# Weight sums of a Strassen-like decoder trunk, built in DRAM by accumulating transfers

## The chip, the cores and the metric

The kernel runs on one core of a Trainium2 chip. The metric is the device time of one execution, in microseconds (us). The engines are TensorE (PE, matmuls), VectorE (DVE), ScalarE (ACT), GpSimd (POOL) and SyncE (SP). Each runs its own instructions in order and waits on semaphores for the others. SP and POOL issue nearly all DMA transfers, SP the loads and POOL the stores, each in its own queue; 16 DMA engines carry them out.

## The reference

Sequence 1024, width D = 1024, float32. One normalised input h is projected by one weight matrix `w_in`; two gated linear attentions run on parts of it, each is projected by its own 1024 x 1024 matrix, the two are merged by sigmoid gates, and one output projection follows.

```python
h = rms_norm(x, norm_w[l]) * (1.0 + scale[:, None, :]) + shift[:, None, :]
proj = h @ w_in[l]
hq, hf, hi, hz, gq, gk, gv, gz, ga, mg = jnp.split(proj, IN_OFFSETS, axis=-1)
y_h = hgrn2_branch(hq, hf, hi, hz, lb_all[l], hgrn_norm_w[l])
y_g = gla_branch(gq, gk, gv, gz, ga, gla_alpha_w[l], gla_alpha_b[l], gla_norm_w[l])
u_h = y_h @ w_branch[l, 0]
u_g = y_g @ w_branch[l, 1]
mg = jax.nn.sigmoid(mg.reshape(B, T, N_BRANCH, D_MODEL))
merged = mg[:, :, 0] * u_h + mg[:, :, 1] * u_g
x = x + gate[:, None, :] * (merged @ w_out[l])
```

The weights concerned here are `hi` and `gv` (the values of the two attentions), `mg` (two gates) and `w_branch` (two branches), each 1024 x 1024.

## The kernel before

Large matmuls are done in float32r after each operand has been split in a high and a low part (an ACT copy and a DVE subtraction), as three products hi*hi, hi*lo, lo*hi. The square products of 1024 x 1024 use a scheme of Strassen's kind: the matrix is cut in quadrants, and seven products of half size (`PRODUCTS = (1, 2, 5, 3, 6, 7, 4)`) take the place of eight. Four of the seven (`SUMS`: 5, 6, 3, 7) need sums of weight quadrants:

- 7 is the quadrant (0,0) plus (0,1); 5 is (0,1) plus (1,1); 6 is 7 plus (1,1); 3 is 6 plus (1,0). In the second value stage 3 is formed with the opposite sign.

The order of the work: the norm and the modulation with the first projections (`front`), then a list of jobs that `stream.go` runs: the first value stage (`vjobs[0]`, for gv), the gate features of the first attention, the second value stage (`vjobs[1]`, for hi), and the features of the second attention. The attention itself runs as generators beside the jobs (`weave`): each `yield n` lets n units of matmuls pass. A second track of such generators, `stream.back`, does work ahead of its use, one after another: `alpha_side`, `v_sums`, `prepare`, `gate_side`. At the end come four closing stages (`last_stages`: two gates, two branches) and the output stage.

The weight sums are made by DVE. `v_sums` loads the four quadrants of hi in two halves (kk), makes four results of 128 x 1024 each and stores them in DRAM (`vs_d`). `prepare` does so for the four closing stages: 16 blocks, each loaded in two DMAs of 512 KB (`load_blocks`), four additions of 128 x 512 to half a block's sums each (`weight_sums`: lines L1174, L1176, L1178, L1180; the profile counts 16 of each), and four stores to `w_sums`. Later `load_duo` and `Vjob.load` read the sums back as if they were weights.

The engines' order: PE, ACT and DVE follow the program as written in the first part (`manual_schedule`), and behind it a scheduler of the framework orders each engine's instructions, DMAs included, by what they depend on; `held` keeps marked instructions in the order of the program. A DMA of POOL takes one of eight semaphores in turn, and so waits on POOL for the one eight places ahead in POOL's queue to have landed, as well as for those that it depends on.

Other names that the steps below use: `h` are stores of the modulated input (L257), `qk` stores of the first attention's queries and keys (L365), `fx` stores of combined input quadrants (L1719), `v` stores of value products (L1769) that the attentions load back (L975), `yg` stores of the first attention's result (L889).

Of the kernel before, what the change touches and what calls it, by code (L numbers as in the profile page):

```python
# [16 lines left out]
P = 128  # L17
# [72 lines left out]
def hybrid_trunk_kernel(  # L90
# [1065 lines left out]

    w_sums = [[[dp.tile([P, T], F32, name=f"ws{b}{j}{i}") for i in range(4)] for j in range(2)] for b in range(4)]

    summed_up = set()
    paused = [False]  # L1160

    def load_blocks(b, i):
        src = sources[b][i]
        x = [S.get([4, 2, P]) for _ in range(2)]
        for kh in range(2):
            nc.sync.dma_start(x[kh].rearrange("p k a f -> p k (a f)"),
                              src[kh * 512:(kh + 1) * 512, :].rearrange("(k p) f -> p k f", p=P))
        return x

    def weight_sums(b, i, x1, x2):  # L1170
        s1, s2 = S.get([2, 4, P]), S.get([2, 4, P])
        parts = {5: s1[:, 0], 6: s1[:, 1], 3: s2[:, 0], 7: s2[:, 1]}
        add = nc.vector.tensor_add
        held(add(parts[7], x1[:, :, 0], x1[:, :, 1]))  # L1174
        yield 1
        held(add(parts[5], x1[:, :, 1], x2[:, :, 1]))  # L1176
        yield 1
        held(add(parts[6], parts[7], x2[:, :, 1]))  # L1178
        yield 1
        held(add(parts[3], parts[6], x2[:, :, 0]))  # L1180
        for p, q in SUMS.items():
            nc.gpsimd.dma_start(w_sums[b][i // 2][q][:, i % 2 * 512:i % 2 * 512 + 512],  # L1182
                                parts[p].rearrange("p k f -> p (k f)"))
        S.free(x1, x2)
        S.free(s1, s2, sent=True)
        summed_up.add((b, i))

    def prepare():
        todo = [(b, i) for b in range(4) for i in range(4)]
        blocks_of = {}  # L1190
        for n in range(len(todo) + 1):
            while n < len(todo) and (len(S.free_list) < 11 or paused[0]):
                yield 1
            if n < len(todo):
                blocks_of[n] = load_blocks(*todo[n])
            if n:
                yield from weight_sums(*todo[n - 1], *blocks_of.pop(n - 1))
            yield 7

# [56 lines left out]
    def load_duo(b, p, j):  # L1256

        t = raw_w[b, p, j] = S.get([2, 512])
        if p in SUMS:
            assert {(b, 2 * j), (b, 2 * j + 1)} <= summed_up  # L1260
            nc.sync.dma_start(t.rearrange("p a f -> p (a f)"), w_sums[b][j][SUMS[p]])
        else:
# [432 lines left out]
    v_d = [dp.tile([T, D], F32, name=f"v{s}") for s in range(2)]  # L1695
    vs_d = {p: [dp.tile([P, T], F32, name=f"vs{p}{kk}") for kk in range(2)] for p in SUMS}
    summed_v = set()
# [23 lines left out]
    def v_sums():  # L1721

        add = nc.vector.tensor_add
        for kk in range(2):
            while len(S.free_list) < 9:
                yield 1
            y = {}
            for at_ in ((0, 1), (1, 1), (0, 0), (1, 0)):
                y[at_] = S.get([2, 512])
                nc.sync.dma_start(y[at_], w_block(1, *at_, kk))  # L1730
            yield 9
            e = S.get([2, 512])
            held(add(e, y[0, 1], y[1, 1]))
            yield 2
            held(add(y[0, 0], y[0, 0], y[0, 1]))
            yield 2
            held(add(y[0, 1], y[0, 0], y[1, 1]))
            yield 2
            held(nc.vector.scalar_tensor_tensor(y[1, 0], y[0, 1], -1.0, y[1, 0], ALU.mult, ALU.subtract))
            for p, t in ((5, e), (7, y[0, 0]), (6, y[0, 1]), (3, y[1, 0])):  # L1740
                nc.gpsimd.dma_start(vs_d[p][kk], t.rearrange("p a f -> p (a f)"))
            S.free(y[1, 1])
            S.free(e, y[0, 0], y[0, 1], y[1, 0], sent=True)
            summed_v.add(kk)
            yield 2

# [48 lines left out]
    class Vjob:  # L1795
# [13 lines left out]
        def load(self):  # L1809
# [6 lines left out]
            if p in SUMS:  # L1816
                assert kk in summed_v
                nc.sync.dma_start(self.w_raw.rearrange("p a f -> p (a f)"), vs_d[p][kk])
            else:
                nc.sync.dma_start(self.w_raw, w_block(s, *W_AT[p], kk))  # L1820
# [95 lines left out]
    def front():  # L1916
# [57 lines left out]
```

## Time and profile before

| | |
|---|---|
| median of 3 runs | 1201.08 us (1200.2 to 1201.88) |
| the profiled execution | 1201.55 us, its span 1199.8 us |
| granted TensorE clock | 0.998 of full |
| instructions profiled | 20303 |
| DMA over the span | 221.24 MB, 184 GB/s in the mean |

How to read the lines shown further on: a group has line, engine, operation, out<-in, the shapes and the count, then busy us and the mean ns of one, then the engine's idle time just before it and who ended it. A timeline row has start, duration, engine, line and operation, and in brackets the idle time before it and what ended that. `SPq` is SP's queue of DMA issues. A DMA row has the count, the KB of each and the median us from issue to landing. A wait row names who waited, for whom, and the us in total, the times and the longest.

### The profile page before, as it was taken

The page shows a single profiled execution, that of the slowest core. Times are in us where ns is not written, and L with a number is a line of the kernel's source. Part 1 is how long each engine was busy: PE and PEld are TensorE (multiplying, and loading weights), DVE is VectorE, ACT ScalarE, POOL GpSimd, SP SyncE. Part 2 cuts the span into 40 slices and gives each one's busy share as a digit, 9 for nine tenths or more (in the row PEclk, how much of TensorE's full clock was granted, in tenths as well). Part 3 has the DMA queues.
Part 4 walks back from the last instruction along what each step waited for, and adds up shares of the span by engine and source line. Part 5 has one row for each costly group of instructions (what it writes and reads, how often), then busy time and mean ns, then how long its engine had stood idle before and what let it go on. Part 6 is the DMA issues. An engine that isn't in the chain of part 4 may idle for free.

```text
span 1199.8 us, 20303 instructions
## 1 busy us (share of the span) xinstructions
PE 1170.1 (98%) x8137; PEld 951.0 (79%) x8137; DVE 846.3 (71%) x1270; ACT 584.9 (49%) x860; POOL 124.3 (10%) x257
## 2 busy tenths in 40 slices
PE   7999999999999999999999999999999999999997
PEld 6776777888878688888888878778888888878886
DVE  4745667657664955887897798695553866988994
ACT  5674462673455445334433435456643644444554
POOL 4111111000110211111111010001120000000000
PEclk9999999999999999999999999999999999999999
DMA  9745445155474855665565454255688846335523
GB/s 324 262 173 201 150 161 176 52 178 175 167 273 141 296 195 161 209 210 160 173 197 178 130 203 124 78 169 179 225 312 284 285 152 210 125 108 173 171 99 134
DMA packets 150641, 221.24 MB, mean 184 GB/s; under 512 B 8971, under 2 KB 107329, under 8 KB 150546
## 3 DMA queue, kind: packets, MB, share of 16 engines
q1 hardware_dynamic: 132114, 158.37, 42.4%
q0 software_dynamic: 18384, 61.56, 13.3%
q8 instruction: 64, 1.05, 0.4%
q14 instruction: 31, 0.25, 0.1%
q10 hardware_dynamic: 48, 0.01, 0.0%
HBM read 154.37 MB, written 65.54 MB: 183 GB/s over the span
## 4 chain that ended last, share of the span: by engine, by line
PE 65%; issue 20%; DVE 6%; ACT 4%; DMA 3%; POOL 2%; SPq 0%; POOLq 0%; DVEq 0%; ACTq 0%
PE pd L594 16%; PE pd L1330 11%; PE pd L1879 9%; PE sc_ps L1330 6%; PE pm L1330 6%; PE pd L1507 3%; PE pd L386 2%; PE sc_ps L1507 2%; PE pm L1507 1%; PE pm L798 1%; POOL ws L1182 1%; DVE b L212 1%; PE pm L817 1%; DMA b<-in_ada_w_dram 1%; PE sc_ps L386 1%
## 5 line engine op out<-in xcount | busy, mean ns | idle before, releaser
L594 PE MATMUL pd<-b,b 128*128 128x512 f32 x1632 | 393.8, 396 | 0.2 <-ACT b L1762 0.2
L594 PEld LDWEIGHTS pd<-b,b 128*128 128x128 f32 x1632 | 303.0, 189 | 65.8 <-issue 0.7
L1330 PE MATMUL pd<-b,b 128*128 128x512 f32 x720 | 173.2, 392 | 0.6 <-DVE b L1422 0.4
L1879 PE MATMUL pd<-b,b 128*128 128x512 f32 x672 | 162.7, 396 | 7.1 <-DVE b L1790 3.4
L1330 PEld LDWEIGHTS pd<-b,b 128*128 128x128 f32 x720 | 133.9, 188 | 31.2 <-DVE b L1422 0.9
L1879 PEld LDWEIGHTS pd<-b,b 128*128 128x128 f32 x672 | 123.4, 188 | 40.7 <-ACT b L1762 4.0
L212 DVE TENSOR_TENSOR b<-b,b 128x1024 fp32r<-128x1024 f32 x78 | 94.2, 1222 | 48.4 <-ACT b L211 48.1
L1273 DVE TENSOR_TENSOR b<-b,b 128x1024 fp32r<-128x1024 f32 x56 | 68.2, 1221 | 69.2 <-ACT b L1272 53.0
L1272 ACT CAST b<-b 128x1024 fp32r<-128x1024 f32 x56 | 58.4, 1050 | 65.0 <-PE pm L1330 18.1
L211 ACT CAST b<-b 128x1024 fp32r<-128x1024 f32 x78 | 79.8, 1047 | 6.4 <-PE pd L1879 3.0
L1330 PE MATMUL sc_ps<-b,b 128*128 128x512 f32 x324 | 78.7, 391 | 0.4 <-ACT b L1302 0.4
L1330 PE MATMUL pm<-b,b 128*128 128x512 f32 x300 | 72.1, 389 | 0.0
L1330 PEld LDWEIGHTS sc_ps<-b,b 128*128 128x128 f32 x324 | 60.4, 188 | 13.9 <-ACT b L1302 1.1
L1249 ACT CAST b<-b 128x1024 fp32r<-128x1024 f32 x48 | 49.7, 1050 | 43.9 <-PE pd L1330 15.9
L1250 DVE TENSOR_TENSOR b<-b,b 128x1024 fp32r<-128x1024 f32 x48 | 57.7, 1219 | 18.4 <-ACT b L1249 12.2
L1330 PEld LDWEIGHTS pm<-b,b 128*128 128x128 f32 x300 | 56.3, 188 | 11.7
L203 DVE TENSOR_TENSOR b<-b,b 128x1024 fp32r<-128x1024 f32 (+1 forms) x36 | 35.1, 983 | 29.5 <-ACT b L202 29.4
L386 PE MATMUL pd<-b,b 128*128 128x512 f32 x192 | 52.3, 405 | 2.8 <-DVE b L362 1.9
L1182 POOL DMA_DIRECT2D ws<-b x64 | 34.9, 546 | 193.6 <-DVE b L1174 107.4
L703 ACT COPY xb<-b 128x512 f32<-128x512 f32 x48 | 29.7, 621 | 50.8 <-PE sc_ps L683 23.8
L817 PE MATMUL pm<-scT,b 128*128 128x128 f32 x256 | 46.9, 275 | 0.0
L386 PEld LDWEIGHTS pd<-b,b 128*128 128x128 f32 x192 | 34.4, 188 | 15.4 <-DVE b L362 2.9
(317 smaller groups left out, 1699.6 us busy)
## 6 DMA issues: line engine op xcount, KB each, us to landing
b<-in_w_in_dram SPq DMA_DIRECT2D x72, 512.0 KB, 4.3
ws<-b POOLq DMA_DIRECT2D x64, 256.0 KB, 3.9
b<-ws SPq DMA_DIRECT2D x32, 512.0 KB, 4.4
b<-in_x_dram SPq DMA_DIRECT2D x16, 512.0 KB, 4.4
b<-in_ada_w_dram SPq DMA_DIRECT2D x32, 256.0 KB, 6.5
v<-b POOLq DMA_DIRECT2D x32, 256.0 KB, 3.7
b<-v SPq DMA_DIRECT2D x16, 512.0 KB, 5.2
b<-fx SPq DMA_DIRECT2D x16, 512.0 KB, 4.5
```

What stands on the lines that cost most here:

```text
L211: held(nc.scalar.copy(hi, src))
L212: nc.vector.tensor_sub(lo, src, hi.bitcast(F32))
L386: nc.tensor.matmul(accs[f], wg(a, d, f), b[d][:, half * 512:half * 512 + 512], start=(d == 0 and n == 0), stop=(d == KT - 1 and n == 2))
L594: nc.tensor.matmul(ps[0:w, th * 512:(th + 1) * 512], a[:, k, 0:w], b[:, th * 512:(th + 1) * 512], start=(k == 0 and n == 0), stop=(k == KT ...
L817: nc.tensor.matmul(o, vch(ch)[:, vh * P:(vh + 1) * P], scT[:, ch, :], start=True, stop=(ch == 0))
L1249: nc.scalar.copy(hi, src)
L1250: nc.vector.tensor_sub(lo, src, hi.bitcast(F32))
L1272: nc.scalar.copy(hi, t)
L1273: nc.vector.tensor_sub(lo, t, hi.bitcast(F32))
L1330: nc.tensor.matmul(o, a[:, sl], c, start=(p in (1, 5) and kt == 0 and n == 0), stop=(kt == 3 and n == 2), skip_group_check=True)
L1507: nc.tensor.matmul(o, a, b, start=(p in (1, 5) and kt == 0 and n == 0), stop=(kt == 3 and n == 2), skip_group_check=True)
L1879: nc.tensor.matmul(st.bank[i], x_, w_, start=(p in (1, 5) and kk == 0 and a == 0 and n == 0), stop=(kk == 1 and a == 1 and n == 2), skip_g ...
```

## The change

The DVE additions of `v_sums` and `weight_sums` go, and with them their loads and stores through SBUF. In their place POOL issues DMAs from DRAM to DRAM: a copy of the first quadrant into the sum's tile, then a DMA with `accum_op=ALU.add` that adds the second to it there; 6 and 3 begin as copies of the finished 7 and 6. `w_sums` becomes one tile of 128 x 4 x 512 for each stage and product. `v_sums` no longer makes 3 with the opposite sign, so the job that uses it splits it with a factor of -1 (`minus_split`). `v_sums` now stands ahead of `alpha_side`, whose delay goes from 72 to 32.

```diff
+    def minus_split(src):
+        hi, lo = (S.get(list(src.shape[1:]), F32R) for _ in range(2))
+        held(nc.scalar.activation(hi, src, AF.Copy, scale=-1.0))
+        nc.vector.scalar_tensor_tensor(lo, src, -1.0, hi.bitcast(F32), ALU.mult, ALU.subtract)
+        return hi, lo
...
-    w_sums = [[[dp.tile([P, T], F32, name=f"ws{b}{j}{i}") for i in range(4)] for j in range(2)] for b in range(4)]
+    w_sums = [{p: dp.tile([P, 4, 512], F32, name=f"ws{b}{p}") for p in SUMS} for b in range(4)]
...
-    def load_blocks(b, i):
...
-    def weight_sums(b, i, x1, x2):
...
+    CHAIN = ((7, (0, 0)), (7, (0, 1)), (5, (0, 1)), (5, (1, 1)), (6, 7), (6, (1, 1)), (3, 6), (3, (1, 0)))
 
     def prepare():
...
+        for b in range(4):
+            def block(kh, a, b=b):
+                src = sources[b]
+                return [src[i][kh * 512:kh * 512 + 512, a * P:a * P + P] for i in range(4)]
+            done = set()
+            for p, src in CHAIN:
+                while paused[0]:
+                    yield 1
+                first = p not in done
+                done.add(p)
+                if isinstance(src, int):
+                    nc.gpsimd.dma_start(w_sums[b][p], w_sums[b][src])
+                else:
+                    for i, x in enumerate(block(*src)):
+                        x = x.rearrange("(k p) f -> p k f", p=P)
+                        y = w_sums[b][p][:, i].rearrange("p (k f) -> p k f", f=P)
+                        if first:
+                            nc.gpsimd.dma_start(y, x)
+                        else:
+                            nc.gpsimd.dma_start(y, x, accum_op=ALU.add)
+                        yield 1
+                yield 4
+            summed_up.add(b)
...
     def v_sums():
...
+        for p, src in CHAIN:
+            first = p not in done
+            done.add(p)
+            for kk in range(2):
+                if isinstance(src, int):
+                    x = vs_d[src][kk]
+                else:
+                    x = w_block(1, *src, kk)
+                y = vs_d[p][kk]
+                if first:
+                    nc.gpsimd.dma_start(y, x)
+                else:
+                    nc.gpsimd.dma_start(y, x, accum_op=ALU.add)
+                yield 2
...
-                self.w = pinned_split(self.w_raw)
+                self.w = minus_split(self.w_raw) if p == 3 else pinned_split(self.w_raw)
...
-        stream.back.append([alpha_side((2, 3)), 72, 1, 0])
         stream.back.append([v_sums(), 2, 1, 0])
+        stream.back.append([alpha_side((2, 3)), 32, 1, 0])
```

What it does to the order of the instructions, at three places. First POOL's queue around the first stores of h. Before, they follow the setup of the masks:

```order
L564 COPY mask16_750<-mask16_750 32x16 x3
L257 DMA h00_112<-b45_225 128x1024
L257 DMA h01_113<-b50_299 128x1024
L257 DMA h02_114<-b55_399 128x1024
L489 MEMSET b69_659 128x512
L491 DMA b69_659<-in_gla_alpha_w_dram 16x512 x4
L567 MEMSET scT_136 128x1024
L257 DMA h03_115<-b62_501 128x1024
```

Now (line L263 is the old L257; L1727 and L1729 are copies and accumulations of `v_sums`, where `vs70` is product 7, half 0; L1187 is a first copy of `prepare`):

```order
L1727 DMA vs60_813<-vs70_817 16x8192
L1729 DMA vs51_812<-in_w_in_dram 256x1x512
L1727 DMA vs61_814<-vs71_818 16x8192
L1729 DMA vs60_813<-in_w_in_dram 256x1x512
L263 DMA h00_112<-b45_225 128x1024
L1729 DMA vs61_814<-in_w_in_dram 256x1x512
L1727 DMA vs30_815<-vs60_813 16x8192
L1187 DMA ws07_774<-in_w_in_dram 128x4x128
L1727 DMA vs31_816<-vs61_814 16x8192
L1729 DMA vs30_815<-in_w_in_dram 256x1x512
L263 DMA h01_113<-b50_299 128x1024
L1729 DMA vs31_816<-in_w_in_dram 256x1x512
```

The value stage's transfers, and from there on those of the closing stages, have moved ahead of and between the stores of the first part. Second, POOL's queue at the stores of the first value stage's sixth product, which the first attention loads. Before:

```order
L1719 DMA fx40_769<-b123_1317 128x1024
L1769 DMA v0_825<-b135_1405 128x512
L1769 DMA v0_825<-b136_1422 128x512
L1769 DMA v0_825<-b135_1405 128x512
L1719 DMA fx41_770<-b124_1318 128x1024
L1769 DMA v0_825<-b136_1422 128x512
```

Now (L1757 is the old L1769, L1713 the old L1719; `ws37` is stage 3, product 7; L1189 accumulates, L1181 copies a sum):

```order
L1757 DMA v0_809<-b135_1403 128x512
L1757 DMA v0_809<-b136_1421 128x512
L1189 DMA ws37_786<-in_w_branch_dram 128x4x128
L1757 DMA v0_809<-b135_1403 128x512
L1187 DMA ws35_783<-in_w_branch_dram 128x4x128
L1713 DMA fx41_770<-b124_1312 128x1024
L1757 DMA v0_809<-b136_1421 128x512
L1187 DMA ws35_783<-in_w_branch_dram 128x4x128 x3
L1189 DMA ws35_783<-in_w_branch_dram 128x4x128 x3
L1757 DMA v0_809<-b125_1321 128x512
L1189 DMA ws35_783<-in_w_branch_dram 128x4x128
L1181 DMA ws36_784<-ws37_786 16x16384
```

At this place the sums of three closing stages are already ahead, and those of the last one stand between the stores; 103 of the 120 transfers are ahead of the fourth store shown, and all 120 ahead of the first yg store. Third, DVE where the first block's additions of a closing stage stood, in the first attention's fourth head. Before:

```order
L1174 TENSOR_TENSOR b_3685<-b_3560 128x512
L1176 TENSOR_TENSOR b_3684<-b_3560,b_3561 128x512
L1178 TENSOR_TENSOR b_3684<-b_3685,b_3561 128x512
L711 TENSOR_TENSOR b_3357<-b_3357,tot_759 128x8x64
L712 TENSOR_TENSOR b_3355<-b_3355,tot_759 128x8x64
L756 COPY_PREDICATED blk<-mask_750,sc_ps 128x8x16
L1180 TENSOR_TENSOR b_3685<-b_3684,b_3561 128x512
```

Now (lines 6 higher):

```order
L212 TENSOR_TENSOR b_3649<-b_3437,b_3648 128x1024
L717 TENSOR_TENSOR b_3339<-b_3339,tot_759 128x16x32
L717 TENSOR_TENSOR b_3339<-b_3339,tot_759 128x8x64
L718 TENSOR_TENSOR b_3337<-b_3337,tot_759 128x8x64
L762 COPY_PREDICATED blk<-mask_750,sc_ps 128x8x16
```

The attention's own operations stand there alone.

More of the change, by code (lines that the diff above doesn't have):

```diff
@@ L1188, in prepare @@
-    def prepare():
[L1189 to L1198, printed above, removed]
+    CHAIN = ((7, (0, 0)), (7, (0, 1)), (5, (0, 1)), (5, (1, 1)), (6, 7), (6, (1, 1)), (3, 6), (3, (1, 0)))
@@ L1695, in hybrid_trunk_kernel @@
     v_d = [dp.tile([T, D], F32, name=f"v{s}") for s in range(2)]
-    vs_d = {p: [dp.tile([P, T], F32, name=f"vs{p}{kk}") for kk in range(2)] for p in SUMS}
+    vs_d = {p: [dp.tile([P, 2, 512], F32, name=f"vs{p}{kk}") for kk in range(2)] for p in SUMS}
     summed_v = set()
@@ L1721, in v_sums @@
     def v_sums():
-        add = nc.vector.tensor_add
-        for kk in range(2):
[L1725 to L1743, printed above, removed]
+        done = set()
+        for p, src in CHAIN:
[12 more added lines that the diff above has]
+                yield 2
+        for kk in range(2):
             summed_v.add(kk)
-            yield 2
+        yield 2
     class Vstage:
```

28 lines of the change are left out of this document (3 added, 25 removed).

## Prediction

> **What bounds the kernel now.** I read the page's busy shares first, then busy time by stretch and PE's waits where the removed additions stand, and last the DMA queues and the timelines of POOL and SP, because the change swaps DVE work for DMA work on POOL's queue.
>
> ```profile
> span 1199.8 us, 20303 instructions
> PE 1170.1 (98%) x8137; PEld 951.0 (79%) x8137; DVE 846.3 (71%) x1270; ACT 584.9 (49%) x860; POOL 124.3 (10%) x257
> ```
>
> PE is busy for 98% of the span, DVE for 71%. The profiled execution took 1201.55 us with this span in it; the median of the runs shown is 1201.08. The sum below is made against 1201.55. Now the stretches (busy us of each engine, granted clock, DMA share, GB/s):
>
> ```profile
> core 0: us, PE busy (x) PEld busy (x) DVE busy (x) ACT busy (x) POOL busy (x), PEclk, DMA share, GB/s
> 0.00:10.00 10.00, 6.01 (x27) 5.64 (x28) 3.92 (x11) 5.64 (x10) 9.35 (x36) 1.00 0.83 235
> 10.00:50.00 40.00, 36.83 (x192) 27.37 (x192) 23.82 (x49) 20.42 (x39) 5.64 (x23) 1.00 1.05 355
> 50.00:100.00 50.00, 49.80 (x252) 36.65 (x251) 23.16 (x48) 35.36 (x57) 11.21 (x18) 1.00 0.51 177
> 100.00:200.00 100.00, 93.56 (x512) 72.12 (x511) 69.87 (x81) 46.61 (x60) 16.07 (x30) 1.00 0.48 167
> 420.00:700.00 280.00, 279.78 (x2604) 233.98 (x2603) 213.24 (x382) 114.09 (x182) 44.09 (x81) 1.00 0.58 183
> ```
>
> Two things are to be seen. From 10 to 50 us the 16 DMA engines are full (share 1.05), so bytes added there push back loads that PE waits for in order. And from 420 to 700 us, where the sums of the closing stages are made, PE is busy for 279.78 of 280 us. PE's waits (us in total, times, longest), the only one of 420 to 700 us, and then the two largest of 700 to 840 us:
>
> ```profile
> PE pd L594 <- ACT b L1762: 0.2, 1, 0.2
> ```
>
> ```profile
> PE sc_ps L652 <- DVE xb L648: 1.9, 1, 1.9
> PE sc_ps L683 <- DVE blk L666: 1.3, 1, 1.3
> ```
>
> **The change part by part.** *Removed: 72 DVE operations.* Two kinds of the four in the closing stages' sums, and two of the four in the value stage's:
>
> ```profile
> L1178 DVE TENSOR_TENSOR b<-b,b 128x512 f32<-128x512 f32 x16 | 11.1, 692 | 0.0
> ...
> L1174 DVE TENSOR_TENSOR b<-b 128x512 f32<-128x512 f32 x16 | 11.0, 687 | 0.0
> L1733 DVE TENSOR_TENSOR b<-b,b 128x1024 f32<-128x1024 f32 x2 | 2.4, 1220 | 0.0
> ...
> L1735 DVE TENSOR_TENSOR b<-b,b 128x1024 f32<-128x1024 f32 x2 | 2.4, 1218 | 0.0
> ```
>
> That is 64 x 0.69 + 8 x 1.22 = 54 us of DVE work. PE waits 0.2 us in the stretch that holds most of it: matmuls hide it already. The two DVE waits just behind, 1.9 + 1.3 = 3.2 us, may go, since DVE gets there with less in hand. The bounds are 0 and 5 us of gain; I take 4. SP loses 40 block loads and POOL 72 stores of sums that go with the additions; those of the closing stages lie in the same covered stretch, and all of them count nothing. The split with a factor of -1 (third product, value stage) is one ACT and one DVE operation of the same shapes in place of two plain ones, twice: nothing, under DVE's idle 29%. The alphas' side work waits 32 units behind value sums that yield 34, so it starts at 66 units instead of 72: nothing.
>
> *Added: 120 transfers from DRAM to DRAM in POOL's queue.* A closing stage has 8 copies and 16 accumulations of 0.262 MB and 2 copies of 1.049 MB, 8.39 MB in all, and there are four; the value stage has 8 copies and 8 accumulations of 0.524 MB, again 8.39 MB. Written: 5 x 8.39 = 41.9 MB, of which 5 x 4.19 = 21.0 MB accumulate. Prices:
>
> ```profile
> q1 hardware_dynamic: 132114, 158.37, 42.4%
> ...
> b<-in_ada_w_dram SPq DMA_DIRECT2D x32, 256.0 KB, 6.5
> ...
> b<-in_w_in_dram SPq DMA_DIRECT2D x24, 256.0 KB, 3.7
> ```
>
> The first row gives the engines' rate: 158.37 MB in 0.424 x 1199.8 = 509 us, 311 GB/s. So 0.262 MB is 0.84 us of all 16 engines, and the 41.9 MB are 135 us if every transfer were a plain copy. No row shows an accumulation. Below it is bounded by a plain copy, 0.84 us; above by the landing of a 256 KB load amid full engines, 6.5 us, as if nothing ran beside it (undisturbed such loads land in 3.7). An accumulation must also read what it adds to, so it is nearest to two plain passes: I take 1.69 us for 0.262 MB, which adds 21.0 MB / 311 GB/s = 67 us and makes 202 us of engine work. The Trainium skill ("Collectives: The Full Stack", section "The bandwidth ceiling: the fold count and why AG ≠ RS ≠ AR") says that the adder itself costs nothing and its second source read does, with a measured ratio of 1.93 to a copy. By that ratio the 67 would be 63 and the time 1302; no run here shows it yet.
>
> *Where they stand.* The change's rows of POOL show it: the transfers need nothing from the compute engines, so they stand from the program's first microseconds on, between the stores of h, qk, fx and v, and all are ahead of the first yg store. Each step of a sum waits on POOL for the step before it to land, and every store behind it in the queue waits too. Where POOL and SP stand now:
>
> ```profile
> 28.17 0.59 POOL L257 DMA_DIRECT2D h<-b  x1 [13.23 <-ACT b L252]
> ...
> 172.50 0.54 POOL L1769 DMA_DIRECT2D v<-b  x1
> ...
> 199.63 0.54 POOL L1769 DMA_DIRECT2D v<-b  x1 [1.78 <-ACT b L1762]
> 259.31 1.08 POOL L889 DMA_DIRECT2D yg<-b  x2 [59.14 <-DVE b L999]
> ```
>
> ```profile
> 185.97 0.96 SPq L975 DMA_DIRECT2D b<-v  x2
> ```
>
> SP's load of v at 185.97, the last row, needs the store of 172.50, 13 us earlier, and SP's queue is in order: behind this load stand the weights of the next matmuls. SP already waits for stores of v, before such weights (us in total, times, longest):
>
> ```profile
> SPq L576 <- DMA v<-b: 20.9, 3, 7.7
> ```
>
> *The sum at two points.* By the shares above, the engines have done 8.3 + 42.0 + 25.5 + 0.48 x 72.5 = 111 us of work by 172.50, and 124 by 199.63. At the v store of 172.50, 103 transfers stand ahead; the 17 behind it (12 accumulations, 3 small and 2 large copies) are 29 us, so 173 are ahead. With the engines always full that store comes at 111 + 173 = 284, 111 late, less 13 of slack: 98 us on SP. At the last v store only 4 accumulations, 7 us, are behind: 124 + 195 = 319, 119 late; its data are not loaded soon, but the halves of buffers that these stores free are. The delay lies between 98 and 119; I take 108. The start is part of this, not extra: the value stage's 16 transfers, 12.6 MB with the second read, are 40 us of engine work, nearly all of it ahead of the second h store, in the full stretch. Nothing recovers it later, since PE is busy throughout. The sum: 1201.55 + 108 - 4 = 1306. POOL's own issue time (count, busy us, mean ns of one) is covered by these waits:
>
> ```profile
> L1182 POOL DMA_DIRECT2D ws<-b x64 | 34.9, 546 | 193.6 <-DVE b L1174 107.4 <-DVE b L1180 26.2 <-DVE b L1178 18.3
> ...
> L357 POOL DMA_DIRECT2D wga<-in_w_in_dram x1 | 1.0, 958 | 0.0
> ```
>
> The second has as many small rows as any of the new ones; 120 x 0.55 to 0.96 us is 66 to 115 us, under the 319.
>
> **The rivals.** *Accumulating is as cheap as copying.* Then 135 us of work: the v store at 111 + 116 = 227, 54 late, less 13 is 41 on SP; the last one 56 late; the middle, 48, gives 1246. Against it: an accumulation reads twice. If only the start paid (40 us) and everything later found slack, the time would be 1238; the 13 us ahead of the v load speak against that.
>
> *Accumulating is much dearer than two passes.* Each further pass over the 21.0 MB adds 67 us: 1373 with one, 1440 with two. At the upper end, 6.5 us for each 0.262 MB, the accumulations take 64 x 6.5 + 8 x 13 = 520 us instead of 134, and the time is 1306 + 386 = 1692. For it: rows of 512 bytes, and chains in which one transfer waits for the landing of another. Against it: two or more chains are in flight at once, and even 30 steps in series (6 in each of five sums) at 6.5 us are 195 us, less than 319.
>
> *The transfers are hidden, and the kernel is faster.* The gain then stands alone: 1201.55 - 4 = 1198. It decides at the v load: the engines' idle time until then is 172.5 - 111 + 13 = 75 us, so the 103 transfers would have to cost under 75 us, while plain copies alone make 116, or 101 at the 355 GB/s of the full stretch. The shares of 0.51 and 0.48 from 50 us on speak for it, the lack of room by a third against it. The Trainium skill ("DMA: Bandwidth & Descriptors", section "Issuing engines are not separate DMA queues") speaks against it as well: transfers issued by any engine end up on the same 16 and interleave.
>
> **How the numbers follow.** Full engines and about two passes (1275 to 1400): 0.58. Cheap accumulation or only the start (1230 to 1275): 0.17. Dear accumulation (over 1400): 0.20. Hidden: 0.05, most of it faster. I predict the likeliest, 1306. The range 1243 to 1440 reaches from just under the cheap case to two more passes; about 0.05 hidden, 0.04 below and 0.11 above are left out. Faster or slower counts from 0.2%, what a measurement of this kernel can tell from no change: faster 0.04, same 0.01, slower 0.95.
>
> **What would show it.** DMA share near 1 from 5 to some 300 us; the SP load of v near 285; the last v store near 310 to 320; new PE waits in the first 65 us that lead back to loads of ada_w, and one or two of tens of microseconds from 100 to 300 us that lead to a POOL store; DVE busy down by some 54 us with nothing gained for it between the first yg stores and the end. The prediction is wrong if DMA is idle while POOL waits (landing time bounds the chains, not bytes), or if PE runs on while the v stores are late.

## The result, and the profile after

The changed kernel takes 1315.05 us (median of 4 runs, 1314.08 to 1317.65) against 1201.48 for the kernel before on the same chip: ratio 1.0946, 95% interval 1.0933 to 1.096. The prediction was 1306 with a range of 1243 to 1440. The profiled execution has a span of 1312.9 us, 113.1 more than the 1199.8 of before.

The page of the changed kernel: span and busy times, DMA share in 40 slices, and the two big DMA queues (q1 is SP's, q0 POOL's; packets, MB, share of 16 engines over the span).

```profile
span 1312.9 us, 20091 instructions
PE 1187.9 (90%) x8137; PEld 961.4 (73%) x8137; DVE 800.2 (61%) x1198; ACT 588.8 (45%) x862; POOL 208.9 (16%) x305
...
DMA  9999999999222456422211221435569776534533
...
q1 hardware_dynamic: 113042, 137.39, 33.2%
q0 software_dynamic: 51600, 82.54, 25.2%
```

The same row of the kernel before, in slices of 30 us:

```profile
DMA  9745445155474855665565454255688846335523
```

DMA is full for ten slices of 33 us, the first 328 us, where before it was full for one. DVE's busy time falls by 46 us (846.3 to 800.2) and not by 54, because the page counts a stretch in which two operations overlap once. Added up one by one from the traces, the durations of DVE's operations fall from 925.8 to 872.2 us, by the 54 that the 72 operations took. PE has the same 8137 matmuls and is busy 17.8 us longer. The stretches of the changed kernel (busy us of each engine, granted clock, DMA share, GB/s) show where PE stops:

```profile
core 0: us, PE busy (x) PEld busy (x) DVE busy (x) ACT busy (x) POOL busy (x), PEclk, DMA share, GB/s
10.00:50.00 40.00, 21.81 (x86) 15.63 (x86) 14.20 (x29) 11.84 (x22) 16.59 (x39) 0.71 1.08 316
50.00:100.00 50.00, 40.82 (x194) 28.93 (x198) 20.41 (x44) 22.15 (x42) 20.42 (x26) 0.85 1.07 288
100.00:200.00 100.00, 60.61 (x259) 44.30 (x252) 29.52 (x43) 35.10 (x47) 53.95 (x61) 0.80 1.09 263
200.00:260.00 60.00, 54.51 (x219) 42.17 (x217) 34.14 (x32) 26.00 (x33) 36.67 (x38) 0.94 1.14 240
260.00:330.00 70.00, 37.90 (x369) 29.57 (x370) 28.47 (x52) 13.77 (x23) 29.15 (x34) 0.76 1.05 226
330.00:540.00 210.00, 204.95 (x1535) 166.02 (x1534) 131.32 (x212) 115.66 (x159) 15.52 (x29) 1.00 0.42 135
```

From 10 to 330 us PE is busy for 215.65 of 320 us; from 330 us on it is as full as before. All of the loss lies in the first quarter of the kernel, and the whole of the transfers too. PE's four largest waits (us in total, times, longest), and below them DVE's wait that stands behind the first:

```profile
PE pd L392 <- DVE b L368: 38.6, 2, 36.7
PE pd L1867 <- DVE b L1778: 24.0, 3, 22.9
PE pm L302 <- DMA b<-in_ada_w_dram: 21.5, 4, 11.4
PE pm L782 <- DVE b L717: 10.3, 1, 10.3
```

```profile
DVE b L368 <- DMA qk<-b: 37.6, 1, 37.6
```

L302, the modulation's matmuls, waits for weights that land late. L392, the matmuls that make the first attention's queries and keys, waits for DVE to empty their accumulators (L368), and DVE waits 37.6 us for a store of qk to leave its buffer. That store stands in POOL's queue behind the sums: the last stores of qk ahead of it go out from 114.47 us, the next from 175.89. In the 53 us ahead of 175.89 POOL is busy with issuing for 25 and waits for landings of sums in the rest, as in the first of these two rows:

```profile
136.63 0.52 POOL L1181 DMA_DIRECT2D ws<-ws  x1 [13.78 <-DMA ws<-in_w_in_dram]
...
175.89 2.69 POOL L371 DMA_DIRECT2D qk<-b  x3
```

L1867, the products of the first value stage, waits 22.9 us in the same way from 258 us on: DVE stands there behind ACT (L211), whose idle time the page puts down to stores of v, 18.3 us of it at this place:

```profile
L211 ACT CAST b<-b 128x1024 fp32r<-128x1024 f32 x76 | 77.7, 1047 | 27.4 <-DMA v<-b 21.5
```

The places that the prediction named, on SP's and POOL's timelines (start, duration), and two waits of SP:

```profile
288.02 6.56 SPq L981 DMA_DIRECT2D b<-v  x2
```

```profile
272.71 0.54 POOL L1757 DMA_DIRECT2D v<-b  x1 [0.92 <-DMA ws<-in_w_branch_dram]
...
307.21 2.22 POOL L1757 DMA_DIRECT2D v<-b  x4
313.82 5.16 POOL L1189 DMA_DIRECT2D ws<-in_w_branch_dram  x4 [4.39 <-DMA ws<-ws]
```

```profile
SPq L582 <- DMA v<-b: 23.3, 2, 18.7
...
SPq L981 <- PE pd L1867: 8.2, 1, 8.2
```

The load of v at 288.02 was itself released last by a matmul (8.2 us). SP's long wait for a store of v, 18.7 us, stands one load of weights earlier (L582).

In the table below each matmul of a kernel is put beside the same matmul of the kernel before (the n-th of its line), and the difference of their starts is taken, in us; the head of a column is the matmul's time in the kernel before. It is worked out from the traces. All the experiments are in it.

| kernel | 51 | 112 | 124 | 185 | 221 | 671 | 711 | end |
|---|---|---|---|---|---|---|---|---|
| the change | 32 | 33 | 73 | 102 | 118 | 116 | 112 | 113 |
| value_only | 25 | 26 | 26 | 28 | 31 | 41 | 37 | 36 |
| closing_only | 22 | 46 | 83 | 105 | 105 | 104 | 101 | 107 |
| copy_for_add | 19 | 24 | 37 | 49 | 63 | 61 | 57 | 60 |
| quarter_bytes | 5 | 27 | 50 | 50 | 53 | 51 | 47 | 52 |
| stores_on_sp | 38 | 40 | 43 | 51 | 69 | 67 | 64 | 67 |
| sp_and_copies | 30 | 32 | 47 | 52 | 55 | 53 | 49 | 52 |
| closing_late | 26 | 26 | 26 | 27 | 30 | 27 | 24 | 38 |
| closing_late_value_dve | 0 | 0 | 1 | 3 | 4 | 4 | 1 | 9 |
| late_copies | 0 | 0 | 1 | 1 | 1 | 1 | -2 | 1 |
| late_faster | 0 | 0 | 1 | 2 | 2 | 76 | 73 | 71 |
| late_faster_own_marks | 0 | 0 | 1 | 2 | 2 | 79 | 75 | 74 |

The change loses 32 us before 51, 39 at one place (112 to 124, the wait for qk), 29 up to the v load and 16 behind it; it gains 3.6 between 671 and 711, just behind the sums of before, and loses 1 after. By the trace of the kernel before, 1.9 of the 3.6 are PE's wait for DVE at 704.6 us, and most of the rest is the granted clock, which stands at half from 706.1 to 709.5, right behind that wait. The control `stores_on_sp_before`, further down, keeps the additions on DVE and waits 1.5 us at the same place, but its clock stays full there, and it gains 2.0. So about 2 us of the gain are DVE's wait; the rest goes with the clock. (`value_only` keeps the closing sums on DVE too, but there they end at 633 us of the kernel before instead of 698: it loses 6.5 us between 600 and 671 and then gains the same 3.6. The rest of what it loses between 221 and 671 stays unexplained.)

### The profile page after: what moved, and what is told of

Read it like the earlier page. It is cut to its first block, busy times and chain, and to the rows that moved or that the text cites. A ratio compares the mean times of both kernels' runs of the same rounds, so it can differ in the third digit from the quotient of the medians.

```text
span 1312.9 us, 20091 instructions
## 1 busy us (share of the span) xinstructions
PE 1187.9 (90%) x8137; PEld 961.4 (73%) x8137; DVE 800.2 (61%) x1198; ACT 588.8 (45%) x862; POOL 208.9 (16%) x305
## 3 DMA queue, kind: packets, MB, share of 16 engines
q8 instruction: 64, 1.05, 0.3%
## 4 chain that ended last, share of the span: by engine, by line
issue 37%; PE 34%; DMA 18%; POOL 5%; ACT 3%; DVE 2%; SPq 1%; POOLq 0%; ACTq 0%; DVEq 0%
PE pd L1324 10%; PE sc_ps L1324 5%; PE pm L1324 5%; DMA ws<-ws 5%; PE pd L600 4%; DMA ws<-in_w_in_dram 3%; POOL ws L1189 3%; PE pd L1501 3%; DMA b<-in_ada_w_dram 3%; DMA ws<-in_w_branch_dram 3%; PE sc_ps L1501 2%; PE pd L1867 2%; PE pm L1501 1%; DMA fx<-b 1%; DMA qk<-b 1%
## 5 line engine op out<-in xcount | busy, mean ns | idle before, releaser
L600 PE MATMUL pd<-b,b 128*128 128x512 f32 x1632 | 394.5, 397 | 1.6 <-DVE b L212 1.3
L600 PEld LDWEIGHTS pd<-b,b 128*128 128x128 f32 x1632 | 303.2, 189 | 67.7 <-DVE b L212 1.8
L1867 PE MATMUL pd<-b,b 128*128 128x512 f32 x672 | 170.8, 410 | 30.2 <-DVE b L1778 24.0
L1867 PEld LDWEIGHTS pd<-b,b 128*128 128x128 f32 x672 | 129.1, 196 | 66.6 <-DVE b L1778 24.4
L1324 PE MATMUL pd<-b,b 128*128 128x512 f32 x720 | 173.0, 391 | 0.6 <-DVE b L1416 0.4
L1324 PEld LDWEIGHTS pd<-b,b 128*128 128x128 f32 x720 | 133.9, 188 | 30.9 <-DVE b L1416 0.9
L392 PE MATMUL pd<-b,b 128*128 128x512 f32 x192 | 56.1, 427 | 39.5 <-DVE b L368 38.6
L211 ACT CAST b<-b 128x1024 fp32r<-128x1024 f32 x76 | 77.7, 1047 | 27.4 <-DMA v<-b 21.5
L392 PEld LDWEIGHTS pd<-b,b 128*128 128x128 f32 x192 | 36.4, 200 | 54.7 <-DVE b L368 39.5
L895 POOL DMA_DIRECT2D yh<-b x16 | 8.7, 542 | 307.3 <-DVE b L1109 307.2
L956 DVE TENSOR_TENSOR b<-b,pd 128x1024 f32<-128x1024 f32 x24 | 30.0, 1250 | 37.4 <-ACT b L955 37.3
L1189 POOL DMA_DIRECT2D ws<-in_w_in_dram x32 | 43.8, 1945 | 41.9 <-DMA ws<-ws 21.6
```

The source lines that it names most:

```text
L392: nc.tensor.matmul(accs[f], wg(a, d, f), b[d][:, half * 512:half * 512 + 512], start=(d == 0 and n == 0), stop=(d == KT - 1 and n == 2))
L600: nc.tensor.matmul(ps[0:w, th * 512:(th + 1) * 512], a[:, k, 0:w], b[:, th * 512:(th + 1) * 512], start=(k == 0 and n == 0), stop=(k == KT ...
L1189: nc.gpsimd.dma_start(y, x, accum_op=ALU.add)
L1324: nc.tensor.matmul(o, a[:, sl], c, start=(p in (1, 5) and kt == 0 and n == 0), stop=(kt == 3 and n == 2), skip_group_check=True)
L1867: nc.tensor.matmul(st.bank[i], x_, w_, start=(p in (1, 5) and kk == 0 and a == 0 and n == 0), stop=(kk == 1 and a == 1 and n == 2), skip_g ...
```

## The experiments

Two theories stood against each other. Bytes: the 16 engines are full, the added work of some 200 us pushes everything behind it, and the time follows the work. Queue: a store in POOL's queue waits until the chains of sums ahead of it have landed, and the time follows the number of steps and their landings, not the bytes. The expectations below split the second in two: the landing theory, in which the steps' landings alone set the time, and the order theory, in which only stores that stand behind the sums cost. Each time below is the median of 2 to 10 executions; behind it stand its ratio to the kernel before on the same chip and the ratio's interval.

**One half alone.** `value_only` takes the new `v_sums` and leaves `prepare` on DVE; `closing_only` the other way round.

> The kernel before with the value stage's transfers alone (16 of the 120); the closing stages' sums stay on DVE. Bytes theory (the time is lost because the 16 DMA engines have no room): by the packets of the changed kernel's trace these 16 transfers are 33 us of engine work, all in the full first 50 us, so 1201 + 30 = about 1232. Rival, landing theory (steps of a sum wait for each other's landing, whatever their size): 8 steps in series at 9 us are 72 us that the stores of h wait for, so 1240 to 1270. Rival, order theory (the engines have room, only stores stuck behind transfers in POOL's queue cost): the stores of h are late but not needed before 78 us, so 1203 to 1212.

> The kernel before with the closing stages' transfers alone (104 of the 120); the value stage's sums stay on DVE. Bytes theory: 190 us of engine work; the last v store comes at 124 + 190 - 9 = 305, 105 late, so 1285 to 1305. Landing theory: four sums of six steps in series at 9 us, 216 us, end near 225, so 1220 to 1235. Order theory: as the bytes theory, 1285 to 1315.

Measured: 1237.86 us (ratio 1.0298, 1.0268 to 1.0328) and 1307.51 (1.0878, 1.0844 to 1.0911). `value_only` lies 6 us above the bytes theory's 1232, 2 below the landing theory's range and 26 above the order theory's. `closing_only` rules the landing theory out (at most 1235); it lies in the order theory's range and 2.5 above that of bytes, which is nearly the same, so it does not tell these two apart. The two losses, 36 and 106, are 142 together and 113 in the change: they overlap. The value stage's 16 transfers cost 25 us by 51 us, and the wait behind it is the one for late weights:

```profile
PE pm L302 <- DMA b<-in_ada_w_dram: 17.2, 4, 10.8
```

The closing stages' transfers carry the rest, though their results are not read before 766 us of the kernel before. In `closing_only` a small load of POOL, that of the alphas' weights, became a place of its own:

```profile
PE pd L392 <- DVE b L368: 37.0, 2, 35.0
PE pm L906 <- DMA b<-in_gla_alpha_w_dram: 21.4, 1, 21.4
```

**Copies in place of accumulations.** Every transfer stays, with its place and its chain, but none accumulates (the sums are left out).

```diff
-                            nc.gpsimd.dma_start(y, x, accum_op=ALU.add)
+                            nc.gpsimd.dma_start(y, x)
...
-                    nc.gpsimd.dma_start(y, x, accum_op=ALU.add)
+                    nc.gpsimd.dma_start(y, x)
```

> The changed kernel with every accumulation replaced by a plain copy, so the weight sums are left out (the sums' tiles hold the last quadrant copied). Number, order and chains of the 120 transfers stay. Bytes theory: plain copies from POOL are merged to packets of 4 KB, 0.67 us of 16 engines for 0.262 MB against 2.2 for an accumulation, so the work falls from some 222 to 105 us: the v store of 172.50 at 111 + 91 = 202, 30 late, less 13; the last one 26 late; 1215 to 1245. Landing theory: steps in series as before, 1290 or more.

Measured: 1260.4 us (1.0486, 1.0455 to 1.0517). Both ranges miss: 15 us above the bytes theory's, 30 below the landing theory's. So 55 us of the 113 are the price of accumulating in place of copying, and 59 remain with plain copies. The page of `copy_for_add` shows the same bytes in POOL's queue as the change, in fewer packets and less time:

```profile
span 1259.4 us, 20091 instructions
...
q0 software_dynamic: 21904, 82.54, 18.6%
```

0.252 x 1312.9 - 0.186 x 1259.4 = 331 - 234 = 97 us of all 16 engines, for 72 accumulations.

**A quarter of the bytes.** Each of the 120 transfers moves a quarter of its data, in the same order and the same chains (the rest of each sum is left out, and the loads of sums read the quarter four times).

```diff
-                    nc.gpsimd.dma_start(w_sums[b][p], w_sums[b][src])
+                    nc.gpsimd.dma_start(w_sums[b][p][:, :, 0:128], w_sums[b][src][:, :, 0:128])
...
-                        x = x.rearrange("(k p) f -> p k f", p=P)
-                        y = w_sums[b][p][:, i].rearrange("p (k f) -> p k f", f=P)
+                        x = x[0:P, :]
+                        y = w_sums[b][p][:, i, 0:P]
```

> The changed kernel with a quarter of the bytes in each of the 120 transfers (128 of each 512 columns; the rest of each sum is left out, and the loads of sums read the quarter four times). Number, order and chains stay. Bytes theory: some 60 us of engine work, under the 75 us of idle engines ahead of the v load; only the start pays, some 8 us: 1205 to 1220. Landing theory: 1280 or more. Order theory: landing times fall with the bytes, but stores still stand behind chains: 1215 to 1250.

Measured: 1253.5 us (1.0428, 1.0398 to 1.0459). The bytes theory missed by 33 us: three quarters of the work gone, and 52 of the 113 us are still there. The order theory's 1215 to 1250 is 3.5 too low, the landing theory's 1280 is 26 too high. The stretches of this kernel, and its two largest waits:

```profile
10.00:50.00 40.00, 33.55 (x165) 23.69 (x164) 23.30 (x47) 18.96 (x36) 26.03 (x54) 0.91 1.13 338
50.00:100.00 50.00, 30.81 (x149) 22.12 (x148) 17.05 (x41) 20.67 (x36) 41.42 (x61) 0.80 0.83 176
100.00:200.00 100.00, 77.18 (x328) 58.68 (x327) 39.51 (x42) 38.98 (x51) 46.87 (x70) 0.88 0.67 190
```

```profile
PE pd L392 <- DVE b L368: 22.1, 2, 20.2
PE pm L906 <- DMA b<-in_gla_alpha_w_dram: 19.0, 1, 19.0
```

The first 51 us cost 5 in place of 32, so the loss there is bytes. From 50 to 200 us the engines have room (0.83, 0.67), and still PE loses 22 us to the load of the alphas' weights and 23 to the store of qk: both stand in POOL's queue behind chains of sums. That is the queue's loss, seen by itself. It is not made of landings alone. POOL's rows ahead of the alphas' load:

```profile
77.50 6.74 POOL L1189 DMA_DIRECT2D ws<-in_w_in_dram  x8
...
90.78 2.25 POOL L497 DMA_DIRECT2D b<-in_gla_alpha_w_dram  x4
```

From 60.5 us to this load POOL is busy for 28 of 30 us: it issues one transfer after another, 0.84 us each in the first row, and hardly waits. By these rows PE's 19.0 us are for the most part POOL's own time to issue, which neither theory had. Ahead of the store of qk, from 107.5 to 157.7 us, POOL is busy for 30 of 50 us and waits for landings in most of the rest. No run parts the two.

**The stores off POOL.** The stores of h, qk, fx and v and the alphas' load go through SP's queue, in the changed kernel and, as a control, in the kernel before.

```diff
-            nc.gpsimd.dma_start(h_d[half][i], hT[half, i].rearrange("p a t -> p (a t)"))
+            nc.sync.dma_start(h_d[half][i], hT[half, i].rearrange("p a t -> p (a t)"))
...
-            nc.gpsimd.dma_start(v_d[self.s][r:r + P, f * 512:f * 512 + 512], t)
+            nc.sync.dma_start(v_d[self.s][r:r + P, f * 512:f * 512 + 512], t)
```

> The changed kernel with the 60 stores of h, qk, fx and v and the load of alpha_w issued by SP instead of POOL (and the clearing of alpha_w's buffer on DVE), so that no store of the first part stands behind a transfer; transfers, their bytes and their start stay. Bytes theory (no room in the engines): loads and stores still share full engines for some 300 us, 1290 to 1320. Order theory (what costs is standing behind transfers that wait on POOL): only the fight for the engines in the first 65 us stays, about 30 us, and some waits behind: 1235 to 1265.

> The control: the kernel before with the same 60 stores and the load of alpha_w on SP. Both theories: POOL's queue is no bound there, so 1197 to 1206.

Measured: 1269.88 us (1.0574, 1.0552 to 1.0595) for the changed kernel, 1202.91 (1.001, 0.9999 to 1.0022) for the control. The move itself costs nothing that can be told, and it takes 46 us off the change. The order theory's upper end of 1265 is 5 too low; the bytes theory's 1290 is 20 too high. PE's two waits in question (38.6 and 24.0 in the change) are nearly gone, and the one for weights has grown:

```profile
PE pm L302 <- DMA b<-in_ada_w_dram: 25.4, 5, 11.0
...
PE pd L1867 <- DVE b L1778: 9.2, 3, 8.1
...
PE pd L392 <- DVE b L368: 4.4, 2, 2.2
```

**Both at once.** Stores on SP and copies for accumulations (sums left out).

> Both edits at once on the changed kernel: stores of h, qk, fx and v on SP, and plain copies for accumulations (the sums are left out). Alone they took 46 and 55 us off the loss of 113. Theory: the two are separate, queue order on the one side and engine work on the other, and add up: 113 - 46 - 55 = 12 left, 1213, range 1208 to 1222. Rival: they overlap (a store waits in POOL's queue because accumulations land late, so the dearer accumulation is most of the queue's cost): the time is 1235 to 1260, near the better of the two single edits.

Measured: 1251.96 us (1.0407, 1.0382 to 1.0431). My theory that the two add up was wrong, and the rival's 1235 to 1260 holds it. Of the 113 us about half or more stay whichever cause is taken away: 52 with a quarter of the bytes, 67 with no stores behind the sums, and still 52 with copies as well. The queue is enough for some 47 us (the quarter-size kernel behind its first 51 us). Full engines are enough for some 50: here no store of the first part stands behind a sum, and the DMA share is 1.05, 1.00, 1.00 and 0.88 in the four stretches from 10 to 260 us; that the 50 are theirs is read from these shares. Together the two cost 113, so the loss can't be split into a sum.

**The same transfers, later.** `closing_late` holds each closing stage's transfers until the place where its sums stood in the kernel before: a store of four cleared numbers into the sums' tiles makes the first copies wait for DVE. `closing_late_value_dve` also takes the value sums back to DVE.

```diff
+            mark = S.get([8])
+            held(nc.vector.memset(mark, 0.0))
+            for p in (7, 5):
+                nc.gpsimd.dma_start(w_sums[b][p][0:1, :, 0:1], mark[0:1, 0:4].unsqueeze(2))
+            S.free(mark, sent=True)
```

> The changed kernel with the closing stages' transfers held back: in each of the four stages a store of four numbers from a freshly cleared buffer into the tiles of products 7 and 5 goes ahead of the first copies, so that they cannot start before the place in the program where the sums were made before. All transfers stay, those of the value stage at the start. Bytes and order theory alike: the 104 transfers now lie beside matmuls with idle engines and cost nothing; what stays is the value stage alone, 1238 as measured, less the gain from DVE: 1232 to 1240. If transfers cost something wherever they stand: 1250 or more.

> As the last one, with the value stage's sums back on DVE: no transfer in the first 400 us. Both theories: the loss is gone and only the gain from 64 DVE operations is left, 1 to 5 us: 1196 to 1201. If transfers cost something wherever they stand: 1205 to 1225.

Measured: 1240.53 us (1.0346, 1.0316 to 1.0375) and 1210.41 (1.0078, 1.0063 to 1.0093). The first is at the upper end of its range; the second misses 1196 to 1201 and lies in that of the rival, by which transfers cost something wherever they stand. The same 104 transfers that cost 106 us at the start cost 9 here; with the value sums in DRAM it is 39, hardly more than the 36 of `value_only`. Neither these nor any of the three below, made to find the 9, beats the kernel before.

**Late, with copies.** As `closing_late_value_dve`, accumulations replaced by copies (sums left out).

> As closing_late_value_dve at its old pace, but each accumulation in the closing stages is a plain copy of the same bytes (the sums are left out). Theory one, late end: the pace is set by the units of matmuls, not by the engines, so the last set still ends near 750 to 771 and the loss at 832 to 872 stays, 1206 to 1211. Rival, engine share: about 100 us of engine work goes (64 accumulations of 0.262 MB at 2.2 against 0.67 us), the shares of 0.70 to 0.92 fall, and the time is 1195 to 1201.

Measured: 1203.91 us (1.0014, 1.0002 to 1.0025), between the two theories' ranges. The pages of `closing_late_value_dve` and then of `late_copies`, where the two kernels differ in nothing but 64 accumulations:

```profile
span 1208.5 us, 20174 instructions
...
q0 software_dynamic: 50128, 78.34, 25.8%
```

```profile
span 1200.5 us, 20174 instructions
...
q0 software_dynamic: 21456, 78.34, 19.1%
```

0.258 x 1208.5 - 0.191 x 1200.5 = 311.8 - 229.3 = 82.5 us for 64: an accumulation of 0.262 MB takes 1.29 us of the 16 engines' packet time more than its copy. It also takes (50128 - 21456) / 64 = 448 packets more: 512 packets, one for each row of 512 bytes, where the copy needs 64. Of the 9 us, 6.5 go with the accumulations (1210.41 to 1203.91). What is left, PE's stretches tell, of `late_copies` first and then of the kernel before:

```profile
700.00:740.00 40.00, 40.00 (x425) 33.43 (x424) 26.52 (x53) 16.73 (x29) 13.39 (x19) 1.00 0.70 215
740.00:780.00 40.00, 40.00 (x419) 33.28 (x418) 30.96 (x55) 19.74 (x31) 7.57 (x11) 1.00 0.55 168
780.00:832.00 52.00, 47.78 (x454) 38.81 (x453) 45.18 (x69) 28.65 (x46) 3.82 (x7) 0.99 0.70 236
```

```profile
700.00:740.00 40.00, 37.90 (x392) 30.08 (x391) 34.95 (x60) 16.59 (x28) 0.00 (x0) 0.96 0.46 149
740.00:780.00 40.00, 39.46 (x418) 32.51 (x418) 30.59 (x53) 18.69 (x30) 1.08 (x2) 1.00 0.26 83
780.00:832.00 52.00, 50.54 (x482) 42.07 (x482) 39.54 (x67) 31.30 (x48) 3.72 (x7) 1.00 0.51 165
```

Without the additions PE loses nothing from 700 to 780, where it lost 2.6 us before; then it loses 4.2 from 780 to 832, where it lost 1.5. The gate's side work follows the sums in the same track; its loads of ada_w now go out among the closing stages' loads, from 777 to 821 us, where they went out from 683 to 703 before. That this late end costs is borne out by the same matching of matmuls: `closing_late_value_dve`, with these loads from 782 to 829, goes from 2.4 ahead at 780 us to 8.8 behind at 872, while `late_faster` below, with these loads from 620 to 675, is 70 behind at both places. The gain of the freed DVE is real and small: 2.6 us of PE's idle time here, 5.7 in `late_faster` (76.2 behind at 671, 70.5 at the end), where all else had 70 us more time. The late end gives it back.

**Late, at twice the pace.** Half as many units of matmuls between the transfers; then the same with the cleared numbers in four small tiles of their own.

```diff
-                        yield 1
-                yield 4
+                        if i % 2:
+                            yield 1
+                yield 2
```

> As closing_late_value_dve (1210.41), but the generator that issues the closing transfers lets half as many units of matmuls pass between them, so its last set should end before some 690 us instead of 771, ahead of the end of the sums of before (698). Theory one: the 11 us lost between 832 and 872 us came from the late end (the gate's side work, which follows in the same track, ran into the closing stages); then the loss goes, the gain of about 6.5 us of freed VectorE waits stays, and the time is 1194 to 1200. Rival, the share of the 16 engines: 178 us of transfers in 200 instead of 350 us fill them from 420 to 650, loads come late there, and the time is 1206 to 1220 with new TensorE waits in that stretch.

> As late_faster (1270.3), but the four cleared numbers whose small stores release a stage's transfers lie in four tiles of their own of 32 bytes a partition, and not in a buffer of the shared pool. In late_faster SP waited once 73 us for such a store, which stood in POOL's queue behind the accumulations of the stage before, to load weights into that buffer, and TensorE then waited 48 us. Theory one, the held buffer: that wait goes with its 66 us, the last set ends near 690 us, ahead of the closing stages, the gate's side work is done before them, and the time is 1195 to 1206. Rival, full engines: DMA share is 0.9 to 1.0 from 420 to 680 us whatever the marks are, weights land late and stores of the second attention wait behind accumulations, and the time stays at 1225 to 1270.

Measured: 1270.3 us (1.0569, 1.0542 to 1.0596) and 1275.76 (1.0615, 1.0593 to 1.0638). I expected up to 1200 and up to 1206, so these are two misses; the rivals' 1206 to 1220 and 1225 to 1270 are also too low. The last set did end earlier, at 681 us, and the loss from 832 to 872 did go, as theory one had it; what it lacked is a new loss from 500 to 700 us. The traces show why. SP's largest waits of `late_faster` and of `late_faster_own_marks`:

```profile
SPq L582 <- DMA ws<-b: 73.1, 1, 73.1
```

```profile
SPq L1102 <- DMA yh<-b: 61.5, 1, 61.5
SPq L1055 <- DMA yh<-b: 47.3, 1, 47.3
```

First SP waits 73 us for a buffer whose store, that of the cleared numbers, stands behind the sums on POOL. With that store's buffer out of the way, SP waits just as long for the buffers of yh, the next stores in the same queue. Whatever store comes behind the chains takes the part. Stretches of `late_faster`:

```profile
500.00:600.00 100.00, 82.66 (x798) 68.92 (x796) 49.34 (x90) 31.98 (x54) 49.33 (x50) 0.93 0.97 177
600.00:700.00 100.00, 49.70 (x499) 39.94 (x499) 45.79 (x74) 17.45 (x29) 36.74 (x37) 0.73 0.88 190
```

As soon as the sums are asked for faster than the engines land them (share 0.97), POOL's queue grows, and PE loses 67.6 us in 200.

## Why the prediction was right, and where it was not

*The total.* 1306 against 1315, within 1275 to 1400, the case that was taken as likeliest. The delay was taken as 108 and is 118 at its height and 116 before the gain; the gain was taken as 4 and is 3.6, by the matched matmuls between 671 and 711. That the 4 comes so near is partly luck: it was made of two waits for DVE, 1.9 and 1.3. The first is gone and the clock's 1.7 behind it; at the place of the second nothing is gained.

*The two points.* SP's load of v, predicted near 285, starts at 288.02; it is 102 late, for 98. The last v stores, predicted at 310 to 320, go out from 307.21. The 172.50 store, predicted at 284, goes out at 272.71. The 98 was 111 of the store less 13 of slack; the store is 100 late, and the load comes 15 us behind it, as it came 13 behind it before. No slack was used up, because SP was held by an earlier store of v and then by a matmul. An error of 11 and one of 13 cancel here: the figure is luck, that stores of v hold up SP's loads is not.

*The start is part of the delay, not extra.* Right: the lag is 32 by 51 us, 40 us of engine work were put there, and nothing is added to the 102 to 118 later. Alone the value stage's transfers cost 36, beside the 1238 of the rival in which only the start pays: 1237.86.

*The price of an accumulation.* This term was too small. I took 0.84 us over a copy for 0.262 MB; measured are 1.29 with rows of 512 bytes. The 8 of 0.524 MB with rows of 2 KB take the remaining 97 - 82.5 = 14 us, 1.8 each or 0.9 for 0.262 MB, as predicted; this is an estimate, since the 82.5 comes from another pair of kernels. So the accumulations' extra is 97 us and not 67. The copies' price was about right: against the 13.3% of 1199.8 us of before, less the 64 stores that went (16.8 of 61.56 MB, 44 us by their share), the 33.6 MB of `late_copies` are 229 - 160 + 44 = 113 us, an estimate, 0.88 for 0.262 MB. The Trainium skill ("Collectives: The Full Stack", section "The bandwidth ceiling: the fold count and why AG ≠ RS ≠ AR") gives a measured ratio of 1.93 between a step that adds and one that copies; by these estimates the 2 KB rows here agree, (1.76 + 1.8) / 1.76 = 2.0, and the 512-byte rows do not: (0.88 + 1.29) / 0.88 = 2.5. The measurement decides.

*What made up for it.* The sum took a share of 1.00 as full. The stretches show 1.05 to 1.14, because packets of one engine overlap. By the rows shown and the 0.82 of the first 10 us, the engines had done 8 + 43 + 54 + 109 + 68 + 13 = 296 us of work by 272.71: 4% more than the 284 of the sum, done at a mean share of 296 / 272.71 = 1.08. Two errors of 4 and 8% stood against each other.

*POOL's own issue time.* It was taken as 0.55 to 0.96 us for each transfer, 66 to 115 us, and as covered by the waits. By the trace POOL is busy with the 120 transfers for 129 us, because an accumulation with 512 rows takes at least 1.24 us to issue and a copy of the same bytes 0.74. In the change this is under the 319, as predicted; in the quarter-size kernel it is what the alphas' load waits for.

*The cause.* Half right. I named full engines as what moves the v stores, and took the wait of a store behind the landings of chains as a detail of it. The sign against it that the prediction named, idle DMA while POOL waits, does not come up in the changed kernel, whose share stays near 1; but the quarter-size kernel has room in its engines from 50 us on (0.83, 0.67) while POOL issues or waits, and takes 52 us longer than the kernel before. A forecast from bytes alone would have given that kernel 1205 to 1220 where it takes 1253.5. The number came out, as far as the shares tell, because in the kernel as it stands the engines are full all the same: a landing that a store waits for is then itself a matter of bytes. The same failure made me expect that `late_faster` would gain.

*The rivals.* Cheap accumulation was put at 1246; with copies in their place the kernel takes 1260.4, so that rival was 14 too low. Dear accumulation: dearer by half, nowhere near a whole further pass. Hidden: not there at the start, and nearly so with the transfers spread from 420 to 771 us, which cost 9 us with accumulations and 2 with copies.

## What to carry to other kernels

A DMA that needs nothing goes out as soon as its queue lets it, long before anyone needs its result; placed there it takes the engines from loads that are needed now (the 104 closing transfers: 106 us at the start, 9 when spread over the covered stretch). In a queue that issues in order, a chain of dependent transfers holds up each store behind it, and through the store's buffer the loads of another queue: count the stores behind a chain and the time that the queue's engine takes to issue it, not the bytes alone. And before moving work off an engine, read what that engine's waits cost: 54 us of VectorE work stood beside 2 to 6 us of lost TensorE time.

## What the runs showed of the hardware that was not expected

- An accumulating transfer goes row by row, 512 packets for 0.262 MB in rows of 512 bytes; a plain copy of the same rows by POOL goes in 64. POOL takes at least 1.24 us to issue the first and 0.74 us to issue the second.
- The granted clock falls where PE waits, with no work added to it: 0.71 from 10 to 50 us, 0.80 from 100 to 200, 0.76 from 260 to 330, and 1.00 behind. In the trace of the change it is at half in nine pieces of the first 331 us, 3.4 to 37.5 us long, each a multiple of 3.4 and 119 us together, and full from there to 1310 us. The products of the value stage are slower for it. The groups of the kernel before, and then of the changed one:

```profile
L1879 PE MATMUL pd<-b,b 128*128 128x512 f32 x672 | 162.7, 396 | 7.1 <-DVE b L1790 3.4 <-ACT b L1762 1.3 <-DVE b L212 0.6
```

```profile
L1867 PE MATMUL pd<-b,b 128*128 128x512 f32 x672 | 170.8, 410 | 30.2 <-DVE b L1778 24.0 <-DVE b L212 2.6 <-ACT b L211 1.7
```

  Of the 113 us, 17.8 are matmuls that take longer, not waits (PE busy 1187.9 against 1170.1). The Trainium skill ("TensorE: Matmul & The Clock Gate", section "What's actually happening") says that the clock halves after an idle window of about 3.4 us and comes back with work; the stretches agree, in that only those with long waits lie under 1.00. In the kernel before, a wait of 1.9 us was enough once (half clock from 706.1 to 709.5), and in the control a wait of 1.5 us at the same place was not.
- The share of the 16 engines can read over 1, and a higher share can move less: 1.14 at 240 GB/s with the accumulations from 200 to 260 us, against 1.05 at 355 GB/s from 10 to 50 us before.
